# A two-layer decoder on one core: ten instead of seven weight tiles lead with their first token half in the second layer, shared large tiles in SBUF, and sums of squares on VectorE

## The chip, the core and the metric

The kernel runs on one core of a Trainium2 chip. The core has five engines with instruction streams of their own: TensorE (PE, matrix products into PSUM), VectorE (DVE), ScalarE (ACT), GpSimd (POOL) and SyncE (SP), which here only issues transfers between HBM and SBUF. The metric is the device time of one execution in microseconds (us), lower being better. A kernel is timed by the median of several executions; beside these, one execution was taken by the hardware profiler, and all views quoted below are of that one.

## The reference

A decoder of two layers runs over 528 tokens: 16 learned meta tokens ahead of a sequence of 512, each 1024 wide. The meta tokens are removed at the end. Everything is float32.

```python
for i in range(DEPTH):                                    # 2 layers
    m = _mixer(_rmsnorm(h, pre_mix_norm[i]), pos, w_in[i], ...)
    h = h + _rmsnorm(m, post_mix_norm[i])
    f = _conv_ffn(_rmsnorm(h, pre_ffn_norm[i]), ffn_up[i], ...)
    h = h + _rmsnorm(f, post_ffn_norm[i])
return h[:, N_META:]
...
def _mixer(...):
    rq, rk, rv, rg, gq, gk, gv, gr, ga = jnp.split(h @ w_in, offs, axis=-1)   # 3600 columns
    # retention: 4 heads of 128, rotary on rq and rk, fixed decay, chunkwise states
    # gated linear attention: 4 heads (64 for keys, 128 for values), decay from ga by a rank-16 gate
    merged = concat([headnorm(o_ret) * silu(rg), headrms(o_gla) * silu(gr)])
    return merged @ w_out
...
def _conv_ffn(h, ffn_up, ffn_conv_w, ffn_conv_b, ffn_down):
    a, g = jnp.split(causal_conv3(h @ ffn_up), 2, axis=-1)  # 2 x 2816 columns
    return (gelu(a) * g) @ ffn_down
```

## The kernel before

**Layout.** Activations stand transposed: features on the 128 partitions, tokens along the free dimension. The residual stream is `h`, eight slices (`KD`) of 128 features by 528 tokens (`L`) in float32. Each linear layer runs in float16 pieces: the normalised input `xh` and each weight are split into a high and a low half, and a product of a slice is three matmuls (high x high, low x high, high x low: lines 361 to 363). The tokens are cut in two halves, 0 to 232 and 232 to 528 (`SPLIT`). In layer 1 the first half of some tiles begins at token 14 (`base`), so it is 218 wide there. A weight tile of 128 columns with its eight slices makes 24 matmuls for a token half.

**Weights.** `plan()` lists all weight tiles in the order of use. `block()` hands out a tile and fetches up to ten tiles ahead (`AHEAD`): a load by SP into a staging buffer `st` (line 89), then ACT's high half (line 105) and DVE's low half (line 106) into a `unit`, of which there are ten (`UNITS`).

**Stages.** Each layer has a mixer, an output projection (`out_proj`, tile name po), an up-projection (`ffn_up`, pu) and a down-projection (`ffn_down` in layer 0, pd; `last_down` in layer 1, which works with seven products of quarter matrices). The mixer's projections have the tile name pj and run over 29 tiles in the order of `TILES`: ga, gk x2, gq x2, gv x4, then twice (rk x2, rq x2, rv x2), gr x4, rg x4. Each of them is done for both token halves.

**The lead.** The norm at the end of a layer gives the first token half of `xh` earlier than the second. So `mixer` makes a list `seq`: the first `LEAD` tiles for their first half, then the same tiles for their second half, then the other tiles with both halves in turn. Ahead of the first second half, whatever is left of the generator that makes the second half of `xh` is traced (`self.finish(self.later)`). `ffn_up` does the same with `ULEAD` = 5 pairs of tiles.

**The background.** Everything else of the mixer is written as generators in a list `bg`: `vtr` transposes a value tile, `gla(pr)` is a pair of gated-attention heads, `ret(hd)` a retention head (`ret_scores`: tiles rs and rst; `ret_states`: kv and sn; `head_out`: o, its statistics bst, mv, rs_t, rs_r, the normalised on, and the transposes pto, times the gate, into `merged`). `tick(n)` advances the first generator of the list that isn't waiting by one step, n times. In the mixer each half tile of `seq` ends with `tick(TICK)`, two steps. The two gated generators are spawned behind the second half of gq1, a retention head behind its rq, a transposition of v goes to the head of the list. What is left at the end of `seq` is done by `drain()`, ahead of the output projection. The output projection takes the slices of `merged` in the order 4, 5, 6, 7, 0, 1, 2, 3, so the retention heads last.

**The norm** (`norms`, `token_rstd`, `scaled`). ACT squares the eight slices one after another (line 330), and the squares are added up in `acc` (line 332): on POOL for slices 1 to 6, on DVE for slice 7, or always on DVE where the argument `last` is true. A matmul with ones sums over the partitions (nst, line 316); POOL takes the root (line 300); a matmul spreads it (nbc); DVE multiplies (line 345), POOL adds to `h` (line 347), the squares of the new `h` are summed in the same way, and `scaled` writes `xh` by ACT and DVE (lines 304 and 305).

**Space and order.** The SBUF pools give each tile an address from its life in a simulated run; where no number of buffers is given, the framework chooses it. The same simulated run puts the instructions of each engine in order. The order is kept as written at the start for ACT, DVE and SP (`manual_schedule`), and for the weight loads of layer 1 (`keep_in_program_order`). PSUM has three tiles for projections (`pmm`) and five for everything else (`pmx`). Two places in SBUF are used in turn by several tiles: the tag "xh" by `xh` and by `wrest` (part of the last down-projection's weights), and the pool `gen`, with 41 slots, by nearly all the short-lived tiles.

Of the kernel before, what the change touches and what calls it, by code (L numbers as in the profile page):

```python
# [14 lines left out]
P = 128  # L15
# [28 lines left out]
LEAD = 7  # L44
# [21 lines left out]
CELL = 1056  # L66

# [10 lines left out]
class Block:  # L78
# [8 lines left out]
    def load(self):  # L87
        st = self.st = cell(self.kern.stage, [P, self.nk, self.w], F32, *self.kern.stage_of(self.layer))
        load = self.kern.nc.sync.dma_start(st, self.src[:, self.c0 : self.c0 + self.w].rearrange("(k p) c -> p k c", p=P))
        if self.layer:  # L90
            self.kern.tc.keep_in_program_order(load)

    def fetch(self):
# [6 lines left out]
        if self.w < P:  # L100
            self.unit = cell(self.kern.wpool, [P, self.nk, P // (2 * self.w), 2, self.w], F16, "unit", "unit")
# [10 lines left out]
class Quarter:  # L112
# [21 lines left out]
    def fetch(self):  # L134
# [13 lines left out]
        self.unit = cell(kern.wpool, [P, 2, 2, 512], F16, "unit", "unit")[:, :, : self.nk]  # L148
# [6 lines left out]
class Kern:  # L155
    def __init__(self, ctx, tc, a):
# [5 lines left out]
        self.wpool = pool("wpool", UNITS)  # L162
# [7 lines left out]
        self.rate = 1  # L170

# [29 lines left out]
    def next_xh(self):  # L201
        xh = self.keep.tile([P, KD, 2, L], F16, tag="xh", name="xh", bufs=1)
# [7 lines left out]
    def w11_place(self, kk):  # L210
# [3 lines left out]
        if kk == WFIRST:  # L214
            self.wrest = self.keep.tile([P, HK - WFIRST, 512], F32, tag="xh", name="wrest", bufs=1)
        return self.wrest[:, kk - WFIRST : min(kk + 2, HK) - WFIRST]
# [11 lines left out]
    def constants(self):  # L228
        nc, a, c = self.nc, self.a, self.const
        widths = (("h", KD * L), ("ident", P), ("ones", P), ("mhalf", 10), ("par", NROW), ("pars", 48), ("cvec", 4 * 88), ("ss", 10), ("first", 10),  # L230
                  ("mask", len(LEVELS) * 16), ("decay", 2 * NH * 5), ("sso", 8))
        every = c.tile([P, sum(n for _, n in widths)], F32, name="every")
# [6 lines left out]
        self.decay = self.decay.rearrange("p (a h c) -> p a h c", a=2, h=NH)  # L239
        nc.gpsimd.memset(self.ones, 1.0)  # L240
# [32 lines left out]
    def mixer_constants(self):  # L273
# [4 lines left out]
        nc.sync.dma_start(self.decay, a["c_decay"])  # L278
        yield

    def tables(self):
        nc, a = self.nc, self.a
        self.cosT = self.g([P, L], F32, "cosT")
        self.sinT = self.g([P, L], F32, "sinT")
        self.tri = self.g([P, P + 16], F32, "tri")
        nc.sync.dma_start(self.cosT, a["c_cos"])
        nc.sync.dma_start(self.sinT, a["c_sin"])
        nc.sync.dma_start(self.tri, a["c_tri"])
# [894 lines left out]
```

## Time and profile before

| | before |
|---|---|
| median of three runs | 1273.3 us (1272.73 to 1276.95) |
| the profiled execution's own time | 1271.71 us |
| its span, from the first to the last instruction | 1269.8 us |
| mean granted clock of TensorE | 0.992 |
| HBM read, written | 120.45 MB, 2.10 MB |

The stages by the first matmul of each in the trace:

| stage | from, us | to, us |
|---|---|---|
| start | 0 | 13.7 |
| mixer of layer 0 | 13.7 | 243.7 |
| output projection of layer 0 | 243.7 | 289.8 |
| up-projection of layer 0 | 289.8 | 531.0 |
| down-projection of layer 0 | 531.0 | 653.8 |
| mixer of layer 1 | 653.8 | 879.8 |
| output projection of layer 1 | 879.8 | 923.5 |
| up-projection of layer 1 | 923.5 | 1158.5 |
| last down-projection and end | 1158.5 | 1269.8 |

How a page of the profile reads: its first part has the busy time, share of the span and number of instructions of each engine. "PEld" is the load of weights into TensorE, beside its matmuls. In a group's or an instruction's row, L662 is a line of the kernel, `rs<-rq,rk` the tile written and the tiles read (buffer numbers left out), 128x296 the partitions and elements, and x8 a count. A row of the timeline begins with the time from the start of the span and the length of the stretch, both in us, and may end with the idle time of the engine ahead of it and what ended that, in square brackets. In the table of groups the busy time and the mean in ns of one instruction stand behind the first bar, and the idle time with its releaser behind the second. The clock is the share of its full speed that TensorE was granted.

### The profile page before, as it was taken

To read this page: it belongs to the slowest core of one execution; us is meant where nothing else is said; L and a number is where in the kernel's file an instruction comes from. 1 tells how busy PE (TensorE), PEld (TensorE's weight loads), DVE (VectorE), ACT (ScalarE), POOL (GpSimd) and SP (SyncE) were. 2 spreads that over 40 slices of the span, in tenths; PEclk is the share of its full clock that TensorE was granted. 3 is DMA by queue.
4 is the path that set the end of the run, shared out by engine and by line. 5 is a ranking of instruction groups with operands and counts; after the bars stand their busy time and mean duration, and the time that the engine had idled before them with its cause. 6 is when DMAs were issued, how large, how long until landed. Compare 5 with 4: busy or idle time off the path is not lost.

```text
span 1269.8 us, 26401 instructions
## 1 busy us (share of the span) xinstructions
PE 1239.7 (98%) x11090; PEld 1019.8 (80%) x11090; DVE 819.8 (65%) x1510; ACT 642.0 (51%) x1200; POOL 167.6 (13%) x218
## 2 busy tenths in 40 slices
PE   8999999999999999999988999999999999999997
PEld 6777788888788888888876787888898888886443
DVE  5578845457876666512286688454478867887875
ACT  6664444354855555423255644343548656664541
POOL 1013310044000000000141132100430000000000
PEclk8999999999999999999998999999999999999999
DMA  9731222222433342214152322222215333304651
GB/s 258 212 87 55 68 67 67 68 72 63 133 102 98 101 125 79 88 47 120 32 139 67 84 68 68 64 68 71 84 50 146 108 102 103 126 1 165 200 191 67
DMA packets 206971, 124.26 MB, mean 98 GB/s; under 512 B 6704, under 2 KB 194276, under 8 KB 206852
## 3 DMA queue, kind: packets, MB, share of 16 engines
q1 hardware_dynamic: 206692, 122.04, 32.6%
q8 instruction: 87, 1.43, 0.5%
q0 software_dynamic: 160, 0.52, 0.2%
q14 instruction: 32, 0.26, 0.1%
HBM read 120.45 MB, written 2.10 MB: 97 GB/s over the span
## 4 chain that ended last, share of the span: by engine, by line
PE 80%; DVE 8%; ACT 3%; issue 3%; POOL 2%; DMA 1%; SPq 1%; DVEq 0%; POOLq 0%; ACTq 0%
PE pu L362 12%; PE pu L363 12%; PE pu L361 12%; PE pj L361 6%; PE pj L363 6%; PE pj L362 6%; PE pl L1047 5%; PE pd L362 3%; PE pd L361 3%; PE pd L363 3%; PE po L361 2%; PE po L362 2%; PE po L363 2%; DVE unit L106 2%; PE o L590 1%
## 5 line engine op out<-in xcount | busy, mean ns | idle before, releaser
L362 PE MATMUL pu<-xh,unit 128*128 128x296 f16 (+2 forms) x1408 | 385.7, 275 | 2.0 <-DVE xh L305 2.0
L363 PE MATMUL pu<-xh,unit 128*128 128x296 f16 (+2 forms) x1408 | 385.7, 275 | 0.0
L361 PE MATMUL pu<-xh,unit 128*128 128x296 f16 (+2 forms) x1408 | 384.0, 275 | 0.8 <-ACT xh L304 0.8
L106 DVE SCALAR_TENSOR_TENSOR unit<-st,unit 128x1024 f16<-128x1024 f32 (+1 forms) x186 | 227.5, 1226 | 214.5 <-ACT unit L105 207.8
L361 PEld LDWEIGHTS <-unit 128*128 128x128 f16 x2912 | 285.8, 98 | 48.8 <-issue 5.6
L363 PEld LDWEIGHTS <-unit 128*128 128x128 f16 x2912 | 285.6, 98 | 45.5 <-issue 2.9
L362 PEld LDWEIGHTS <-unit 128*128 128x128 f16 x2912 | 286.3, 98 | 44.5 <-issue 2.2
L105 ACT ACTIVATE unit<-st 128x1024 f16<-128x1024 f32 (+1 forms) x186 | 191.7, 1034 | 138.7 <-PE pu L363 48.7
L361 PE MATMUL pj<-xh,unit 128*128 128x296 f16 (+2 forms) x896 | 248.6, 279 | 1.8 <-ACT gaT L541 1.8
L363 PE MATMUL pj<-xh,unit 128*128 128x296 f16 (+2 forms) x896 | 248.8, 278 | 0.0
L362 PE MATMUL pj<-xh,unit 128*128 128x296 f16 (+2 forms) x896 | 248.6, 278 | 0.0
L934 ACT ACTIVATE u<-pu 128x296 f32<-128x296 f32 (+2 forms) x176 | 66.2, 379 | 99.3 <-PE pu L363 99.2
L363 PE MATMUL pd<-ffa,unit 128*128 128x232 f16 (+1 forms) x352 | 96.8, 276 | 0.0
L361 PE MATMUL pd<-ffa,unit 128*128 128x232 f16 (+1 forms) x352 | 96.8, 276 | 0.0
L362 PE MATMUL pd<-ffa,unit 128*128 128x296 f16 (+1 forms) x352 | 96.7, 276 | 0.0
L332 POOL TENSOR_TENSOR acc<-acc,sq 128x296 f32<-128x296 f32 (+2 forms) x36 | 32.4, 900 | 344.8 <-ACT sq L330 344.1
L300 POOL TENSOR_TENSOR rs_r<-rs_t,every 128x1 f32<-128x1 f32 (+5 forms) x33 | 37.2, 1131 | 279.5 <-DVE rs_t L297 99.5
L923 DVE SCALAR_TENSOR_TENSOR ca<-u,every,ca 128x527 f32<-128x527 f32 (+1 forms) x88 | 66.8, 759 | 10.8 <-ACT ca L918 9.6
L363 PE MATMUL po<-merged,unit 128*128 128x296 f16 (+2 forms) x256 | 69.9, 275 | 0.0
L362 PE MATMUL po<-merged,unit 128*128 128x296 f16 (+2 forms) x256 | 69.9, 275 | 0.0
L923 DVE SCALAR_TENSOR_TENSOR cg<-u,every,cg 128x527 f32<-128x527 f32 (+1 forms) x88 | 66.6, 757 | 4.9 <-ACT cg L918 4.3
L361 PE MATMUL po<-merged,unit 128*128 128x296 f16 (+2 forms) x256 | 69.6, 275 | 0.0
(218 smaller groups left out, 1535.6 us busy)
## 6 DMA issues: line engine op xcount, KB each, us to landing
st<-in_ffn_up SPq DMA_DIRECT2D x88, 512.0 KB, 3.8
st<-in_w_in SPq DMA_DIRECT2D x56, 512.0 KB, 4.0
st<-in_ffn_down SPq DMA_DIRECT2D x46, 512.0 KB, 3.9
st<-in_w_out SPq DMA_DIRECT2D x16, 512.0 KB, 3.6
st<-in_ffn_down SPq DMA_DIRECT2D x8, 384.0 KB, 5.5
out<-yo SPq DMA_DIRECT2D x8, 256.0 KB, 2.0
xt<-in_x SPq DMA_DIRECT2D x6, 256.0 KB, 3.6
w<-in_ffn_down SPq DMA_DIRECT2D x3, 512.0 KB
```

What stands on the lines that cost most here:

```text
L105: nc.scalar.activation(u[:, 0], st, AF.Copy, scale=SW)
L106: nc.vector.scalar_tensor_tensor(out=u[:, 1], in0=st, scalar=SW, in1=u[:, 0], op0=ALU.mult, op1=ALU.subtract)
L300: nc.gpsimd.tensor_tensor(out=r[:w, :n], in0=t[:w, :n], in1=self.mhalf[:w, :n], op=ALU.pow)
L332: eng.tensor_tensor(out=acc[:, :n], in0=acc[:, :n], in1=sq[:, :n], op=ALU.add)
L361: nc.tensor.matmul(ps[:, :n], w[:, 0, kk, :], x[:, 0, n0:n1], start=i == 0, stop=False)
L362: nc.tensor.matmul(ps[:, :n], w[:, 0, kk, :], x[:, 1, n0:n1], start=False, stop=False)
L363: nc.tensor.matmul(ps[:, :n], w[:, 1, kk, :], x[:, 0, n0:n1], start=False, stop=i == tot - 1)
L590: nc.tensor.matmul(o[:, i, :], intra(i), vn(i), start=i == 0, stop=i == 0, skip_group_check=i > 0)
L923: nc.vector.scalar_tensor_tensor(out=to, in0=u[:, max(lo, d) - d : L - d], scalar=self.cvec[:, ci(i) : ci(i) + 1], in1=to, op0=ALU.mult, o ...
L934: nc.scalar.activation(u[:, n0:n1], ps[:, : n1 - n0], AF.Copy, scale=IXW)
L1047: mm = lambda x, w, **kw: nc.tensor.matmul(ps, x, w, skip_group_check=more, **kw)
```

## The change

It has three parts.

*The lead.* `LEAD` becomes a pair: seven tiles lead in layer 0 as before, ten in layer 1 (ga, gk0, gk1, gq0, gq1, gv0 to gv3, rk0).

*Sums of squares.* In `ffn_down` all additions of squares go to VectorE; twelve of them were on GpSimd (six tiles, two token halves). `out_proj` stays as it was.

*Shared tiles.* Tiles that had places of their own or in the pool become views of a few large ones: `xroom` in `every` (the constants' tile) holds `xh`, and at the end `wrest` and `gbc`; `every` also takes `w2`, the staging of the narrow ga tile (`rank`), `tri` (loaded once, with the constants) and the rings of the small tiles rs_t, rs_r and sst. A tile `room` in each mixer holds the keys and queries `kq`, the tables cosT and sinT and the rings of vnt, mv, bst, ms, ont, dgrt and dgt; it has the tag "av", which the activations `av` of layer 0's `ffn_down` use too, now one tile instead of 22 slots. The output of `out_proj`, `m`, becomes one tile, whose place in layer 1 is later used for `late`; the early parts of layer 1's activations share one tile `f`. `ca` and `cg` of `ffn_up` share three buffers and `u` has ten (`2 * ULEAD`). The number of units is stated at each use instead of at the pool, and every unit and staging tile has the full size. The quarter blocks of w11 and t1 from the seventh slice on are fetched at most seven blocks ahead instead of eight.

```diff
-LEAD = 7
+LEAD = (7, 10)
...
+KINDS = (("rs_t", 10, 4), ("rs_r", 10, 4), ("sst", 1, 4))
+MIXKINDS = (("vnt", P, 6), ("mv", 20, 4), ("bst", 6, 8), ("ms", 10, 4), ("ont", P, 8), ("dgrt", 16, 4), ("dgt", 32, 2))
...
     def load(self):
-        st = self.st = cell(self.kern.stage, [P, self.nk, self.w], F32, *self.kern.stage_of(self.layer))
+        if self.w < P:
+            st = self.st = self.kern.rank.rearrange("p (k c) -> p k c", c=self.w)
+        else:
+            st = self.st = cell(self.kern.stage, [P, KD, self.w], F32, *self.kern.stage_of(self.layer))[:, : self.nk]
...
-            u = self.unit = cell(self.kern.wpool, [P, 2, self.nk, self.w], F16, "unit", "unit")
+            u = self.unit = cell(self.kern.wpool, [P, 2, KD, self.w], F16, "unit", "unit", UNITS)[:, :, : self.nk]
...
-        self.ahead = QAHEAD
+        self.ahead = QAHEAD if what not in ("w11", "t1") or kk < WFIRST else min(QAHEAD, WFIRST + 1)
...
     def next_xh(self):
-        xh = self.keep.tile([P, KD, 2, L], F16, tag="xh", name="xh", bufs=1)
+        xh = self.xroom.bitcast(F16).rearrange("p (k i n) -> p k i n", k=KD, i=2)
...
     def sm(self, shape, name, dt=F32, bufs=None):
-        return self.small.tile(shape, dt, tag=name, name=name, **({"bufs": bufs} if bufs else {}))
+        if name not in self.rings:
+            return self.small.tile(shape, dt, tag=name, name=name, **({"bufs": bufs} if bufs else {}))
+        room, at, size, count, used = self.rings[name]
+        self.rings[name][-1] += 1
+        at += used % count * size
+        t = room[: shape[0], at : at + math.prod(shape[1:])]
...
     def tables(self):
-        self.cosT = self.g([P, L], F32, "cosT")
-        self.sinT = self.g([P, L], F32, "sinT")
-        self.tri = self.g([P, P + 16], F32, "tri")
         nc.sync.dma_start(self.cosT, a["c_cos"])
         nc.sync.dma_start(self.sinT, a["c_sin"])
-        nc.sync.dma_start(self.tri, a["c_tri"])
...
     def mixer(self, l):
+        room = cell(self.keep, [P, 6 * L + sum(n * c for _, n, c in MIXKINDS)], F32, "av", "room", 1)
+        self.cosT, self.sinT = room[:, 4 * L : 5 * L], room[:, 5 * L : 6 * L]
+        self.ring(room[:, 6 * L :], MIXKINDS)
-        self.w2 = self.g([P, 256], F32, "w2")
...
-        kq = [cell(self.gen, [P, 2, L], F32, "kq", "kq", 2) for _ in range(2)]
+        kq = [room[:, 2 * L * pr : 2 * L * (pr + 1)].rearrange("p (i n) -> p i n", i=2) for pr in range(2)]
...
-        seq = [(t, 0) for t in TILES[:LEAD]] + [(t, 1) for t in TILES[:LEAD]] + [(t, hf) for t in TILES[LEAD:] for hf in range(2)]
+        lead = LEAD[l]
+        seq = [(t, 0) for t in TILES[:lead]] + [(t, 1) for t in TILES[:lead]] + [(t, hf) for t in TILES[lead:] for hf in range(2)]
         for i, ((nm, h), half) in enumerate(seq):
-            if i == LEAD:
+            if i == lead:
                 self.finish(self.later)
...
-        m = [self.g([P, L], F32, "m") for _ in range(KD)]
+        size = KD * L if l < DEPTH - 1 else HK * 2 * HT
+        self.room = cell(self.keep, [P, size], F32, "m%d" % l, "m", 1)
+        m = self.room[:, : KD * L].rearrange("p (k n) -> p k n", k=KD)
...
         def finish(col):
-            ca = self.g([P, L], F32, "ca")
-            cg = self.g([P, L], F32, "cg")
+            ca, cg = (cell(self.gen, [P, L], F32, "c", nm, 3) for nm in ("ca", "cg"))
...
-                t = self.g([P, 2, L], F16, "ffa")
-                self.split(t, cg[:, lo:], lo, L)
-                av.append(t)
+                if col == 0:
+                    keep["av"] = self.keep.tile([P, KF, 2, L], F16, tag="av", name="av", bufs=1)
+                self.split(keep["av"][:, col], cg[:, lo:], lo, L)
+                av.append(keep["av"][:, col])
...
     def ffn_down(self, l, av):
-        m = [self.g([P, L], F32, "m") for _ in range(KD)]
+        m = self.keep.tile([P, KD, L], F32, tag="m", name="m", bufs=1)
...
-                    self.sumsq(accs[half], ct, m[ct][:, n0:n1], n1 - n0, ct == KD - 1)
+                    self.sumsq(accs[half], ct, m[:, ct, n0:n1], n1 - n0, True)
```

More of the change, by code (lines that the diff above doesn't have):

```diff
@@ L170, in __init__ @@
         self.rate = 1
+        self.rings = {}
     def spawn(self, gen):
@@ L213, in w11_place, with ring @@
             return cell(self.keep, [P, 2, 512], F32, "w11", "w11", WFIRST // 2)
-        if kk == WFIRST:
-            self.wrest = self.keep.tile([P, HK - WFIRST, 512], F32, tag="xh", name="wrest", bufs=1)
-        return self.wrest[:, kk - WFIRST : min(kk + 2, HK) - WFIRST]
+        rest = self.xroom[:, : (HK - WFIRST) * 512].rearrange("p (k c) -> p k c", c=512)
+        return rest[:, kk - WFIRST : min(kk + 2, HK) - WFIRST]
     def sm(self, shape, name, dt=F32, bufs=None):
-        return self.small.tile(shape, dt, tag=name, name=name, **({"bufs": bufs} if bufs else {}))
+        if name not in self.rings:
[4 more added lines that the diff above has]
+        t = room[: shape[0], at : at + math.prod(shape[1:])]
+        names = "abc"[: len(shape) - 1]
+        return t if len(names) == 1 else t.rearrange(f"p ({' '.join(names)}) -> p {' '.join(names)}", **dict(zip(names, shape[1:])))
+    def ring(self, room, kinds):
+        at = 0
+        for name, size, count in kinds:
+            self.rings[name] = [room, at, size, count, 0]
+            at += size * count
     def mm(self, shape, name="mm"):
@@ L229, in constants @@
         nc, a, c = self.nc, self.a, self.const
-        widths = (("h", KD * L), ("ident", P), ("ones", P), ("mhalf", 10), ("par", NROW), ("pars", 48), ("cvec", 4 * 88), ("ss", 10), ("first", 10),
-                  ("mask", len(LEVELS) * 16), ("decay", 2 * NH * 5), ("sso", 8))
-        every = c.tile([P, sum(n for _, n in widths)], F32, name="every")
+        widths = (("h", KD * L), ("xroom", KD * L), ("ident", P), ("ones", P), ("mhalf", 10), ("par", NROW), ("pars", 48), ("cvec", 4 * 88), ("ss", 10), ("first", 10),
+                  ("w2", 256), ("rank", KD * 16), ("tri", P + 16), ("mask", len(LEVELS) * 16), ("decay", 2 * NH * 5), ("sso", 8), ("rooms", sum(n * c for _, n, c in KINDS)))
+        every = cell(c, [P, sum(n for _, n in widths)], F32, "every", "every")
         at = 0
@@ L278, in mixer_constants @@
         nc.sync.dma_start(self.decay, a["c_decay"])
+        nc.sync.dma_start(self.tri, a["c_tri"])
         yield
@@ L552, in v_natural @@
         w = 16 if ret is None else P
-        vnt = self.sm([w, P], "vnt", bufs=6)
+        vnt = self.sm([w, P], "vnt")
         pt = self.mx([P, 4, P], "ptv")
@@ L1032, in last_down @@
         nc = self.nc
-        gbc = [self.g([P, 512], F32, "gbc") for _ in range(2)]
+        c0 = (HK - WFIRST) * 512
+        gbc = [self.xroom[:, c0 + 512 * i : c0 + 512 * (i + 1)] for i in range(2)]
         for i in range(2):
```

32 lines of the change are left out of this document (17 added, 15 removed).

## The prediction, made before the changed kernel was run

> **What bounds the kernel now.** I read the page's first part, then a table of windows around the border of the two layers, then the timelines of single engines there and at the end of layer 1's mixer.
>
> ```profile
> PE 1239.7 (98%) x11090; PEld 1019.8 (80%) x11090; DVE 819.8 (65%) x1510; ACT 642.0 (51%) x1200; POOL 167.6 (13%) x218
> 533.00:553.00 20.00, 20.00 (x205) 19.71 (x202) 4.20 (x6) 4.25 (x10) 1.35 (x2) 1.00 0.09 27
> 566.00:590.00 24.00, 24.00 (x193) 18.65 (x191) 10.55 (x10) 11.80 (x16) 2.27 (x3) 1.00 0.68 179
> 880.00:884.40 4.40, 4.40 (x50) 4.40 (x48) 2.58 (x5) 1.25 (x3) 0.00 (x0) 1.00 0.27 76
> 672.00:677.20 5.20, 2.48 (x18) 1.74 (x17) 2.06 (x8) 1.16 (x3) 0.86 (x1) 1.00 0.00 0
> 677.20:684.10 6.90, 5.93 (x24) 3.43 (x24) 6.90 (x17) 4.46 (x9) 0.00 (x0) 0.51 0.02 4
> ...
> 672.30 0.66 PE L316 MATMUL nst<-every,acc 128*99 128x1 f32 x6
> 677.87 0.40 PE L540 MATMUL pj<-xh,unit 128*128 128x296 f16 x1 [1.69 <-ACT xh L304]
> ...
> 663.58 7.10 POOL L347 TENSOR_TENSOR every<-every,tmp 128x296 f32<-128x296 f32 x8 [3.01 <-DVE tmp L345]
> 681.79 1.60 DVE L305 TENSOR_TENSOR xh<-tmp,xh 128x296 f16<-128x296 f32 x4
> ```
>
> PE is the bound. In a window's row the length comes first, then busy time and count of PE, PEld, DVE, ACT and POOL, then clock, DMA share and GB/s. Windows of one width give the pace: 20.00/205 = 0.098 us for a 232-wide matmul, 24.00/193 = 0.124 for 296, 4.40/50 = 0.088 for 218. There is one real hole. Layer 1 leads with the first token half of seven tiles; they are done at 672. The second half's normalised input `xh` waits for POOL's eight residual adds (7.10 us from 663.58), a reciprocal root and its spreading. PE gets its first piece at 677.87 and the last ends on DVE at 681.79 + 1.60 = 683.4. Worse, the granted clock is 0.51 from 677.2 to 684.1: the idle window is paid for a second time.
>
> **The change part by part.**
>
> *Ten tiles lead in layer 1.* Three more first halves (gv2, gv3, rk0: 3 x 24 = 72 matmuls, all 232 wide) come ahead of the first second half: 72 x 0.098 = 7.0 us. Their weights are there:
>
> ```profile
> L105 ACT ACTIVATE unit<-st 128x1024 f16<-128x1024 f32 (+1 forms) x10 | 9.6, 973 | 8.4 <-PE pd L363 8.4
> ```
>
> that is ACT's group from 625 to 653, the ten units with which layer 1 begins. From 672.0 PE would run the 7.0 us and the small norm and gate matmuls of the window up to 677.2 (2.48 busy), to 681.5, or some 680.9 without their drains. The first 24 second-half matmuls then take 24 x 0.124 = 3.0 us at full clock, to 684: where the trace has done just those (x24 in the row from 677.20) at half clock. So all 72 are free: **-7.0 us**. `xh` may come 2 us later than now at no cost, as one of its eight pieces feeds ten or so matmuls of three open tiles. If a norm matmul stands too early in PE's order, up to 1 us comes back.
>
> *The same edit takes steps away from the background.* Attention runs in generators, and each half tile advances them by two steps. They begin behind gq1's second half. Now 47 half tiles follow from there on, 94 steps; with ten leading, 44, 88 steps. The generators need 90: two of gated attention with 21, four retention heads with 8, eight transposes of v with 2. So the four spare steps go, and the last retention head slips. The trace follows this count:
>
> ```profile
> 848.39 1.16 PE L662 MATMUL rs<-rq,rk 128*128 128x128 f32 x8
> 849.03 0.33 ACT L823 ACTIVATE gr<-pj 128x218 f32<-128x218 f32 x1
> 855.79 0.39 PE L677 MATMUL kv<-vn,kn 128*128 128x128 f32 x2
> 865.13 0.39 PE L677 MATMUL kv<-vn,kn 128*128 128x128 f32 x2
> 868.08 0.38 PE L597 MATMUL o<-vnt,dgrt 128*16 128x128 f32 x2
> 869.19 0.28 DVE L606 BATCH_NORM_STATS2 bst<-o 16x6 f32<-16x128 f32 x1
> 869.78 0.16 DVE L607 BATCH_NORM_AGGREGATE mv<-bst 16x2 f32<-16x6 f32 x1
> 870.60 0.16 DVE L297 TENSOR_TENSOR rs_t<-mv,every 128x5 f32<-128x5 f32 x1
> 870.84 1.28 POOL L300 TENSOR_TENSOR rs_r<-rs_t,every 128x5 f32<-128x5 f32 x1 [5.15 <-DVE rs_t L297]
> 872.15 1.37 DVE L626 TENSOR_SCALAR on<-o,mv,rs_r 128x128 f32<-128x128 f32 x4 [0.53 <-POOL rs_r L300]
> ...
> 879.07 0.60 PE L638 MATMUL pto<-every,on 128*128 128x128 f32 x4
> 879.78 0.89 DVE L641 SCALAR_TENSOR_TENSOR tmp<-pto,every,rg 128x256 f32<-128x256 f32 x2 [2.16 <-ACT rg L823]
> 880.53 0.72 ACT L304 ACTIVATE merged<-tmp 128x256 f16<-128x256 f32 x2
> 881.81 0.77 DVE L305 TENSOR_TENSOR merged<-tmp,merged 128x256 f16<-128x256 f32 x2
> 884.64 0.60 ACT L901 ACTIVATE m<-po 128x218 f32<-128x218 f32 x2 [3.39 <-PE po L363]
> ```
>
> Head 3's scores (848.39) stand right by gr3's first half (849.03), where the count puts them; its states (kv) begin at 855.79 behind rg0's first half, its output ends at 868.46, it is normalised by 873.8 and merely waits for the last gate until 879.07. With 88 steps its scores fall behind rg2's first half, its states behind rg3's first half, its output behind the last projection, its normalising behind everything. Call K the first kv. rg3's second half (24 x 0.124) and a kv end the projections at K + 3.4. kv rounds come 3.1 apart (855.79 to 865.13, three rounds), so the fourth is at K + 9.3 and o ends 3.3 later (865.13 to 868.46): K + 12.6 as paced now, K + 11 or so if rounds shorten once PE runs dry. What PE has meanwhile: sixteen o matmuls (by the rs row 1.16/8 each, 2.3), two kv rounds (0.4), and the output projection, which takes this head last: three open PSUM tiles x 7 of 8 slices x 3 = 63 x 0.088 = 5.5. So PE is dry at K + 11.6. Then follow, one behind another, 0.28, 0.16, 0.16, 1.28, two of the four normalisings 0.7, a transpose pair 0.3, and half of the last three rows before the copy of m (0.45, 0.36, 0.39): 4.1, with some nine handovers of 0.1 (as 870.76 to 870.84), 5.0. I take **+5.2 us** (4 to 7).
>
> *The clock* behind that wait: in the front hole a stretch of 3.4 us with 1.64 busy goes ahead of 6.9 us at 0.51:
>
> ```profile
> 673.80:677.20 3.40, 1.64 (x10) 1.14 (x11) 1.75 (x6) 0.80 (x2) 0.29 (x1) 1.00 0.00 0
> ```
>
> Those 6.9 us are two steps of some 3.4. One costs 1.7 us where PE has work, two 3.4, and part of it falls into the wait itself. I take **+1.0** (0 to 3.4). [...]
>
> *Sums of squares to VectorE* (ffn_down of layer 0).
>
> ```profile
> L332 POOL TENSOR_TENSOR acc<-acc,sq 128x296 f32<-128x296 f32 x6 | 5.8, 964 | 24.7 <-ACT sq L330 24.6
> L332 POOL TENSOR_TENSOR acc<-acc,sq 128x232 f32<-128x232 f32 x6 | 4.1, 675 | 270.9 <-ACT sq L330 270.9
> 641.10 3.47 DVE L332 TENSOR_TENSOR acc<-acc,sq 128x232 f32<-128x232 f32 x4
> 656.78 0.46 DVE L332 TENSOR_TENSOR acc<-acc,sq 128x296 f32<-128x296 f32 x1
> 646.69 0.57 PE L316 MATMUL nst<-every,acc 128*116 128x1 f32 x4 [1.26 <-DVE acc L332]
> ```
>
> Twelve adds move. Nine lie where nothing is late. The last three, of the second token half's tiles 4 to 6, fall at 640 to 646, where DVE's own adds take 0.87 (3.47/4) beside POOL, against 0.46 alone, and PE waits 1.26 for the last. Three more at 0.46 to 0.87 cost 1.4 to 2.6; POOL's absence gives back up to 4 x 0.41 = 1.6. I take **0** (-1.3, the whole wait, to +1.2). [...]
>
> *Shared tiles.*
>
> ```profile
> 653.07 0.35 SPq L287 DMA_DIRECT2D sinT<-in_c_sin  x1
> 653.98 84.73 SPq L89 DMA_DIRECT2D st<-in_w_in  x15
> 1000.00:1100.00 100.00, 100.00 (x921) 87.71 (x919) 74.95 (x100) 59.70 (x100) 0.00 (x0) 1.00 0.39 118
> 659.73 0.85 POOL L300 TENSOR_TENSOR rs_r<-rs_t,every 99x3 f32<-99x3 f32 x1 [10.20 <-DVE rs_t L299]
> 1158.73 3.86 DMA wrest<-in_ffn_down
> ```
>
> Layer 1's `room` (keys, tables, small rings) takes over the space of `av`, which is read until the last down product at 653. Behind its first write in SP's queue, the cosT load, stand sinT and the weight loads. They wait already: sinT goes at 653.07, weights at 653.98. cosT is first needed by rk0 near 680, so 0; if the loads slipped by more than 20 us, each would stall PE. POOL's memset of the keys waits for the same, with 10.20 us of idle time before its next work at 659.73. `rank`, `w2` and `tri` have space of their own (one load fewer): 0. ca and cg share three buffers, so cg's first pass on ACT waits for DVE's product of the column before, with PSUM copies behind it; both engines have slack (59.70 and 74.95 of 100) and three PSUM tiles (24 matmuls of 0.088 each) cover some 6 us. The load of `wrest` (1158.73) waits for the last reader of `xh` as before, or a few matmuls less. Together 0 (-1 to +2).
>
> **Sum**: -7.0 + 5.2 + 1.0 = -0.8 us. The profiled execution took 1271.7 (span 1269.8), the median is 1273.3; so 1270.9 by the first, **1272.5** as a median. A difference of 0.3%, 3.8 us, is about what a measurement of this kernel can tell from none.
>
> **Rivals.**
> 1. *The gain is kept*: head 3 finds enough cover at the end, if the last kv rounds run at 1 us instead of 3.1 and its chain ends under the 5.5 us of output projection. For it: today's head is normalised 5 us before its gate. Against it: the count, which the trace keeps to within a tile. -7.0 + 0.5: 1266.8. Chance 0.28.
> 2. *Slower*: the output projection finds no place in PE's order ahead of head 3's transposes, as today, where pto (879.07) stands before it. Then the 5.5 us of cover go, the wait is 10.7 and two half-speed windows follow: -7.0 + 10.7 + 3.4 = +7.1, less some 1.5 as kv rounds shorten: 1279. It decides from about 20 of the 63 matmuls behind the transposes on. Against it: today's first copy of m only comes at 884.64, behind some 52 po matmuls, so slices of a second and third tile were taken before the first was finished. 0.17.
> 3. *The lead does not do what it says*: PE's order puts the norm's matmuls and `xh` so that PE still waits, and half the 7.0 stays lost: +2.7, 1276. For it: PE waited 1.26 for nst at 646.69. Against it: nst at 672.30 hardly waited. 0.05.
>
> **How the numbers follow.** The forecast has 0.50 and its own range is 1269.5 to 1276.5 by the ends of its terms. Faster by over 0.3% (under 1269.5) is rival 1 and a little of the forecast: 0.30. Slower (over 1277.1) is rival 2 and the upper end of the others: 0.20. Within: 0.50. The range goes from 1265.5 to 1278.5 and leaves out the outer thirds of rivals 1 and 2.
>
> **What would show it.** The windows from 672 to 684 at 0.98 busy or more and a clock of 1.00; rs of the last head behind rg2's first half; a PE wait of 4 to 7 us on merged before po's eighth slice, with a half-speed window behind it. If PE shows no wait there, rival 1 holds; if po stands behind the transposes, rival 2. The prediction is wrong from the ground if layer 1's order follows readiness and not the count of steps.

## The result

The changed kernel takes 1285.26 us (median of four, 1284.51 to 1285.94) against 1273.01 for the one before (1271.69 to 1276.95 in the same comparison): a ratio of 1.0096, 95% interval 1.0078 to 1.0115. The profiled execution has a span of 1283.7 us after 1269.8. The forecast was 1272.5, with a range up to 1278.5; the change is 12 us slower, and outside it.

The first part of the page of the changed kernel, and a view of windows where the hole was (columns as in the prediction):

```profile
PE 1243.5 (97%) x11090; PEld 1021.8 (80%) x11090; DVE 827.8 (64%) x1522; ACT 640.4 (50%) x1200; POOL 160.3 (12%) x206
672.00:677.20 5.20, 5.20 (x56) 5.13 (x55) 1.46 (x6) 0.73 (x2) 0.85 (x1) 1.00 0.02 5
677.20:684.10 6.90, 6.90 (x63) 5.82 (x61) 5.79 (x15) 3.86 (x11) 0.00 (x0) 1.00 0.00 0
```

The hole is filled: both windows are fully busy at full clock, with 119 matmuls in place of 42. So the part of the forecast that was to gain time holds, and the loss is elsewhere. By the first matmul of each stage in the two traces:

| stage, us | before | after | difference |
|---|---|---|---|
| mixer of layer 0 | 230.0 | 232.2 | +2.2 |
| down-projection of layer 0 | 122.8 | 122.2 | -0.6 |
| mixer of layer 1 | 226.0 | 227.4 | +1.4 |
| output projection of layer 1 | 43.8 | 52.0 | +8.2 |
| last down-projection and end | 111.3 | 114.1 | +2.8 |
| the other four together | 536.0 | 535.8 | -0.2 |

The mixer of layer 1 and the projection behind it in three windows: up to the first second half, from there to the first matmul of the output projection, and the output projection. First the kernel before:

```profile
653.80:677.90 24.10, 19.35 (x189) 18.21 (x189) 17.57 (x43) 9.58 (x27) 8.81 (x10) 0.99 0.40 102
677.90:879.80 201.90, 198.60 (x1997) 162.79 (x1997) 132.81 (x347) 97.61 (x199) 34.33 (x50) 0.98 0.26 74
879.80:923.50 43.70, 43.70 (x401) 38.26 (x401) 20.86 (x37) 21.75 (x50) 18.72 (x22) 1.00 0.30 85
```

Then the changed kernel:

```profile
655.20:681.60 26.40, 25.84 (x261) 24.94 (x261) 18.27 (x45) 10.61 (x29) 8.84 (x10) 1.00 0.35 97
681.60:882.60 201.00, 190.44 (x1909) 154.13 (x1908) 128.65 (x327) 95.91 (x194) 35.72 (x49) 0.97 0.26 75
882.60:934.60 52.00, 49.88 (x419) 42.02 (x418) 24.52 (x53) 22.09 (x52) 19.91 (x23) 0.93 0.25 72
```

The first window takes 2.3 us more and holds 72 matmuls more, which are 7.0 us of work: 4.7 us are won there, and 3.4 us more as the half-speed stretch of the hole is gone. **The middle window is the surprise.** It has 88 matmuls fewer (the 72, and 16 of the last head that moved behind it). 201.9 less 7.0 (72 x 0.098), some 2 for the 16, and 3.4 for the clock is 189.5; it takes 201.0. PE's idle time there goes from 3.3 (201.90 - 198.60) to 10.6 us (201.00 - 190.44), which is 7.3 us. And there are half-speed stretches of another kind, three of some 3.4 us, which cost about 5 us together:

```profile
724.60:728.00 3.40, 3.27 (x45) 2.31 (x44) 3.40 (x9) 2.08 (x4) 1.00 (x1) 0.66 0.00 0
790.20:793.60 3.40, 2.41 (x12) 1.50 (x13) 3.37 (x9) 2.15 (x5) 1.18 (x2) 0.55 0.48 144
814.00:820.80 6.80, 6.80 (x46) 5.21 (x45) 0.07 (x1) 2.31 (x10) 0.00 (x0) 0.75 0.01 2
```

Who ends PE's waits is in the view of waits over layer 1's mixer and output projection (behind the colon: us in total, times, longest). In the mixer before, PE's waits on lps from 706 to 782 us come to 0.3 and 0.3; below them the changed kernel's longest three:

```profile
PE lps L738 <- DVE lvx L788: 0.3, 1, 0.3
PE lps L738 <- DVE tots L795: 0.3, 1, 0.3
...
PE lps L756 <- ACT lvx L805: 5.3, 6, 1.6
PE pj L558 <- ACT every L322: 1.7, 1, 1.7
PE pto L656 <- DVE on L644: 1.5, 1, 1.5
```

lps are the level scores of gated attention (`level_scores`): seven levels, each a chain of ScalarE's copy, VectorE's difference (both lvx), GpSimd's and VectorE's multiplications, and PE. They make two stretches, one for each pair of heads. Windows from the first lps of a stretch to the last, before:

```profile
718.20:737.20 19.00, 18.85 (x309) 14.52 (x308) 17.39 (x42) 10.39 (x19) 7.58 (x10) 1.00 0.21 57
761.60:780.00 18.40, 17.22 (x291) 13.13 (x290) 17.78 (x45) 10.71 (x24) 6.28 (x8) 1.00 0.20 59
```

and in the changed kernel:

```profile
721.20:746.60 25.40, 23.34 (x335) 17.53 (x334) 23.07 (x54) 11.38 (x21) 10.73 (x15) 0.93 0.23 64
773.00:795.70 22.70, 17.02 (x281) 12.21 (x280) 19.64 (x47) 8.82 (x16) 10.03 (x13) 0.92 0.16 48
```

The second stretch has ten matmuls fewer than before and lasts 4.3 us longer, 5.7 of its 22.7 us idle. Before, it ran beside rv1, rk2 and the first half of rk3; now it runs beside rq2 and rq3, and the rotary work (`rope`, on VectorE, ScalarE and GpSimd) of rk3 and rq2 falls into it: GpSimd has 10.03 us of work there after 6.28. The first stretch holds 26 matmuls more, and is longer by more than these: 2.1 us of it are idle (25.40 - 23.34). The generators moved against the tiles by several half tiles, and this is what the forecast had not looked at.

The end went as the count had said. In the timelines of PE and the windows around it:

```profile
870.42 1.16 PE L680 MATMUL rs<-rq,rk 128*128 128x128 f32 x8
877.94 0.49 PE L695 MATMUL kv<-vn,kn 128*128 128x128 f32 x2
891.73 1.28 PE L656 MATMUL pto<-every,on 128*128 128x128 f32 x4 [1.50 <-DVE on L644]
893.89 0.71 PE L379 MATMUL po<-merged,unit 128*128 128x218 f16 x3 [0.61 <-ACT merged L322]
...
890.20:893.60 3.40, 1.58 (x6) 0.83 (x6) 2.33 (x7) 0.18 (x1) 1.03 (x1) 0.91 0.00 0
893.60:900.40 6.80, 6.51 (x40) 5.50 (x40) 1.08 (x3) 2.74 (x9) 1.29 (x2) 0.55 0.01 2
```

The last head's scores stand behind rg2's first half, its states behind rg3's, and PE has 63 po matmuls ahead of its transposes. The wait is 1.5 + 0.6 us, and a stretch of 6.8 us at about half clock follows a window that was 1.58 of 3.40 us busy. 2.1 of waiting, some 3.4 of clock and 18 matmuls more (419 after 401) make the 8.2 us.

### The profile page after: what moved, and what is told of

The parts are those of the page before. It is cut to its first block, busy times and chain, and to the rows that moved or that the text cites. A ratio compares the mean times of both kernels' runs of the same rounds, so it can differ in the third digit from the quotient of the medians.

```text
span 1283.7 us, 26385 instructions
## 1 busy us (share of the span) xinstructions
PE 1243.5 (97%) x11090; PEld 1021.8 (80%) x11090; DVE 827.8 (64%) x1522; ACT 640.4 (50%) x1200; POOL 160.3 (12%) x206
## 4 chain that ended last, share of the span: by engine, by line
PE 78%; DVE 10%; DMA 4%; ACT 3%; issue 2%; POOL 2%; SPq 1%; DVEq 0%; POOLq 0%; ACTq 0%
PE pu L380 12%; PE pu L381 12%; PE pu L379 12%; PE pj L379 6%; PE pj L380 6%; PE pj L381 6%; PE pd L379 3%; PE pd L381 3%; PE pd L380 3%; DMA st<-in_ffn_down 2%; PE po L379 2%; PE po L380 2%; PE po L381 2%; PE pl L1072 2%; DVE unit L111 1%
## 5 line engine op out<-in xcount | busy, mean ns | idle before, releaser
L380 PE MATMUL pu<-every,unit 128*128 128x296 f16 (+2 forms) x1408 | 385.4, 274 | 2.1 <-DVE every L323 2.1
L381 PE MATMUL pu<-every,unit 128*128 128x296 f16 (+2 forms) x1408 | 385.4, 274 | 0.0
L379 PE MATMUL pu<-every,unit 128*128 128x296 f16 (+2 forms) x1408 | 383.7, 274 | 0.7 <-ACT every L322 0.7
L111 DVE SCALAR_TENSOR_TENSOR unit<-st,unit 128x1024 f16<-128x1024 f32 x184 | 228.9, 1244 | 170.4 <-ACT unit L110 164.9
L110 ACT ACTIVATE unit<-st 128x1024 f16<-128x1024 f32 x184 | 191.6, 1042 | 157.6 <-PE pu L381 52.7
L379 PE MATMUL pj<-every,unit 128*128 128x296 f16 (+2 forms) x896 | 249.5, 279 | 2.7 <-ACT gaT L559 2.2
L380 PE MATMUL pj<-every,unit 128*128 128x296 f16 (+2 forms) x896 | 249.9, 279 | 0.0
L381 PE MATMUL pj<-every,unit 128*128 128x296 f16 (+2 forms) x896 | 249.5, 279 | 0.0
L381 PE MATMUL pd<-av,unit 128*128 128x232 f16 (+1 forms) x352 | 96.9, 276 | 0.0
L380 PE MATMUL pd<-av,unit 128*128 128x296 f16 (+1 forms) x352 | 96.7, 276 | 0.0
L379 PE MATMUL pd<-av,unit 128*128 128x232 f16 (+1 forms) x352 | 96.7, 276 | 0.0
L350 DVE TENSOR_TENSOR acc<-acc,sq 128x296 f32<-128x296 f32 (+2 forms) x60 | 33.7, 564 | 77.9 <-ACT sq L348 75.6
L318 POOL TENSOR_TENSOR every<-every 128x1 f32<-128x1 f32 (+5 forms) x33 | 37.3, 1135 | 296.1 <-DVE every L315 118.8
L1072 PE MATMUL pl<-unit,fk 128*128 128x512 f16 x330 | 71.5, 379 | 2.8 <-ACT part L1082 2.8
L379 PE MATMUL po<-merged,unit 128*128 128x296 f16 (+2 forms) x256 | 70.9, 280 | 0.6 <-ACT merged L322 0.6
L380 PE MATMUL po<-merged,unit 128*128 128x296 f16 (+2 forms) x256 | 71.4, 280 | 0.0
L381 PE MATMUL po<-merged,unit 128*128 128x296 f16 (+2 forms) x256 | 71.3, 280 | 0.0
```

Source lines behind the costliest of these rows:

```text
L110: nc.scalar.activation(u[:, 0], st, AF.Copy, scale=SW)
L111: nc.vector.scalar_tensor_tensor(out=u[:, 1], in0=st, scalar=SW, in1=u[:, 0], op0=ALU.mult, op1=ALU.subtract)
L318: nc.gpsimd.tensor_tensor(out=r[:w, :n], in0=t[:w, :n], in1=self.mhalf[:w, :n], op=ALU.pow)
L350: eng.tensor_tensor(out=acc[:, :n], in0=acc[:, :n], in1=sq[:, :n], op=ALU.add)
L379: nc.tensor.matmul(ps[:, :n], w[:, 0, kk, :], x[:, 0, n0:n1], start=i == 0, stop=False)
L380: nc.tensor.matmul(ps[:, :n], w[:, 0, kk, :], x[:, 1, n0:n1], start=False, stop=False)
```

## The experiments

Two theories stood at first. **A**: the first halves that lead are missing later as cover, so ten leading tiles cost the time by themselves. **B**: the shared tiles tie the attention's steps together and cause the waits. Each time is a median, with its ratio to the kernel before timed beside it (1272.7 to 1274.6).

**The parts alone.** The lead alone, on the kernel before: `LEAD = (7, 10)`, indexed by the layer.

> The kernel before with ten tiles leading in layer 1 and nothing else changed. Theory A (the three first halves are taken from the work that covers the gated attention's level scores and the end of the mixer): the mixer and output projection of layer 1 take some 9.7 us more than before, as in the changed kernel, so 1273.0 + 9.7 = 1282.7 us; the waits of PE on lps are there again. Theory B (the shared tiles tie the attention's steps together and cause these waits): the gain of 7 us is kept apart from the last head's wait, 1272 to 1275 us, and PE hardly waits on lps.

1279.29 us, 1.0055 (1.0039 to 1.0072). In the profile the mixer and output projection of layer 1 take 228.6 + 51.7, 10.5 more than before; this execution was the slowest of six (1277.57 to 1282.57). The median lies between the two expected numbers, nearer theory A's.

The changed kernel with `LEAD = (7, 7)`:

> The changed kernel with seven tiles leading in layer 1: shared tiles and sums remain. Theory A: mixer and output projection of layer 1 as before (269.7 us together), the hole at 672 to 684 is back; what is left is the start (+2.1), the last stage (+2.8) and the sums (-0.6): 1273.0 + 4.3 = 1277.3 us. Theory B: the waits on lps stay, with the hole beside them: 1273.0 + 4.3 + 9.7 = 1287 us or more.

1277.25 us, 1.0036 (1.0023 to 1.0048). Start and last stage stay long (mixer of layer 0 233.5, last stage 113.6). Its two stretches of level scores last 19.0 and 19.9 us, with no wait on lps over 0.33 us. So theory B falls and A stands. By these two medians the lead costs 6.6 us (1279.29 - 1272.72) and all the rest 4.5 (1277.25 - 1272.72), together 11.1 of the 12.

The sums alone, on the kernel before, and the changed kernel with the sums back on GpSimd:

```diff
-self.sumsq(accs[half], ct, ..., n1 - n0, ct == KD - 1)
+self.sumsq(accs[half], ct, ..., n1 - n0, True)
```

> The kernel before with the twelve additions of squares on VectorE and nothing else. By the stage times of the changed kernel the down-projection of layer 0 gets 0.6 us shorter and the wait for nst (1.26 us before) goes: 1272.4 us. A rival: DVE is late with the normalising behind it, 1273.0 to 1274 us.

> The changed kernel with the twelve additions back on GpSimd. By the stage times: 1285.3 + 0.6 = 1285.9 us, with a wait of some 1.3 us for nst near 646. If the sums matter in layer 1's mixer (DVE work that comes later there), it would be 2 us or more faster than the changed kernel.

1271.01 us, 0.9985 (0.9973 to 0.9996), and 1287.98, 1.0119 (1.0100 to 1.0137): the sums are worth more than the 0.6 us expected. The down-projection takes 121.3 alone (122.8 before), 123.6 with the sums back. In the view of groups over the down-projection, VectorE's adds of the first token half before:

```profile
L332 DVE TENSOR_TENSOR acc<-acc,sq 128x232 f32<-128x232 f32 x8 | 5.8, 731 | 6.8 <-ACT sq L330 6.5
```

and with the sums alone:

```profile
L332 DVE TENSOR_TENSOR acc<-acc,sq 128x232 f32<-128x232 f32 x14 | 6.5, 467 | 44.7 <-ACT sq L330 44.4
```

Six adds more cost VectorE 0.7 us. These means mix adds with and without company. The three adds that ran beside GpSimd's additions of squares, and the three at that place with the sums alone (in ns: shortest, median, longest):

```profile
L332 DVE TENSOR_TENSOR acc<-acc,sq x3: 834/1007/1053, 642.6 to 645.6; 128x232 f32<-128x232 f32 x3
L332 DVE TENSOR_TENSOR acc<-acc,sq x3: 393/399/400, 642.1 to 644.1; 128x232 f32<-128x232 f32 x3
```

The wait for nst is gone. The three adds that run beside GpSimd's additions to `h` take as long with the sums alone as before (0.51, 0.78 and 0.87 us before, 0.50, 0.77 and 0.87 after).

**Where the steps stand.** Ten leading tiles on the kernel before, and more steps for the background early on:

```diff
+early = l == DEPTH - 1 and LEAD[l] + 4 < i < 2 * LEAD[l]
-self.tick(TICK)
+self.tick(2 * TICK if early else TICK)
```

> The kernel before with ten leading tiles, and with four steps of the background instead of two behind the five leading second halves that follow gq1 (ten more steps in all). Theory C (what costs the time is the place of the attention's steps: two more half tiles pass before gated attention begins, its second pair's level scores then fall beside the rotary tiles rk2 to rq3, and the last head slips behind the projections): the output projection of layer 1 is back at 43.8 us, PE's waits on lps near 785 to 790 go, the hole stays filled: 1272.7 - 7 = 1266 us (1264 to 1269). Theory A (the first halves are cover that is missing later, wherever the steps stand): the waits turn up at another place, 1277 to 1281 us.

1269.71 us, 0.9979 (0.9969 to 0.9989). The output projection is back at 43.8 us, the mixer at 223.3. Theory A falls: the cover is not missing everywhere, it depends on where the steps stand. Some of the gain stays lost (1266 was expected, 1269 at most): the stretches last 19.9 and 21.6 us, with a wait of 1.4 in the second. With the sums:

> The same with the twelve additions of squares on VectorE: 1.7 us less than the run before it by either theory, so 1264 us by theory C and 1278 by theory A.

1268.44 us, 0.9964 (0.9952 to 0.9977).

Next, ten leading tiles with rv2 and rv3 ahead of rk2, rk3, rq2 and rq3 in layer 1:

```diff
+TILES = (TILES, TILES[:15] + [TILES[i] for i in (19, 20, 15, 16, 17, 18)] + TILES[21:])
```

> The kernel before with ten leading tiles, and in layer 1 the value tiles rv2 and rv3 ahead of rk2, rk3, rq2 and rq3. The steps are as many as in the kernel with the lead alone, and the last head still ends behind 63 matmuls of the output projection; only what stands beside the second pair's level scores changes (rv tiles, which ScalarE empties, in place of rotary tiles, which VectorE and GpSimd work on). If the neighbours matter, the waits of that stretch (5.4 us and a half-speed window of 1.7) go: 1279.3 - 6 = 1273 us. If only the count does, it stays near 1279.

1274.03 us, 1.0010 (1.0001 to 1.0020). The middle window and the second stretch with the lead alone, then the middle window and both stretches of this kernel:

```profile
681.20:882.00 200.80, 188.81 (x1918) 153.40 (x1916) 130.21 (x330) 95.89 (x195) 35.20 (x49) 0.99 0.26 75
773.90:796.90 23.00, 17.35 (x281) 12.22 (x280) 19.98 (x47) 8.82 (x16) 9.63 (x13) 0.93 0.16 47
...
681.20:872.40 191.20, 185.13 (x1908) 151.97 (x1907) 126.68 (x327) 95.32 (x193) 34.33 (x49) 1.00 0.28 78
720.80:746.10 25.30, 21.80 (x334) 16.82 (x334) 23.00 (x53) 11.29 (x21) 10.70 (x15) 1.00 0.23 64
772.60:790.20 17.60, 17.09 (x293) 13.04 (x292) 15.96 (x40) 9.45 (x20) 6.65 (x8) 1.00 0.21 61
```

The middle takes 191.2 us after 200.8, near the 189.5 worked out above: all but two of the lost microseconds come back by an order of tiles alone (one of them because ten matmuls less stand in the window). The first stretch stays as long as it was, so they come back in the second stretch and behind it. The reason was not quite the expected one. The second stretch starts behind rv3 and runs beside rk2 and rk3, not beside value tiles; but the work of rq2 and rq3 is out of it, and GpSimd has 6.65 us there. The end stays long (output projection 53.1).

Eight leading tiles:

> The kernel before with eight leading tiles. One half tile of 2.4 us goes into the hole, the last head's output stands ahead of rg3, so the output projection stays at 43.8 us. Without a loss in between: 1272.7 - 2.4 = 1270.3 us, 1 or 2 less if it also spares a half-speed window. If the second pair's level scores beside rotary tiles cost what they did with ten (5 to 7 us): 1275 to 1277.

1278.61 us, 1.0043 (1.0031 to 1.0056), more than either number. In its profile the hole is not gone (waits of 1.3 and 1.0 us at 676 and 678, half clock from 680 to 685) and the second stretch is already long (24 us). A little lead has the cost and not the gain.

Both edits of the order in one: rv2 and rv3 first, and three steps beside the gr tiles of layer 1 (`TICK + 1 if l and nm == "gr" else TICK`), on the kernel before with the sums, and on the changed kernel:

> The kernel before with ten leading tiles, rv2 and rv3 ahead of rk2 to rq3, three steps in place of two beside the gr tiles of layer 1 (eight more in all), and the squares' additions on VectorE. In the order of its instructions the last head is done at rg2. The mixer of layer 1 takes 218.0 + 2.5 (the last head's matmuls come back from the output projection), the output projection 43.8 us: 264.3 in place of 269.8, and 1.5 less for the sums: 1272.9 - 7 = 1266 us. If the extra steps put the retention heads too close together, waits of 2 to 4 us on their states: 1268 to 1270.

> The changed kernel with the same two edits of the order (rv2 and rv3 first, three steps beside the gr tiles of layer 1). If the place of the attention's steps is what the ten leading tiles cost, its mixer and output projection of layer 1 come to about 265 us in place of 279.4: 1285.3 - 14.5 = 1271 us; what is then left against the best order of the kernel before, 4 to 6 us, belongs to the shared tiles (start and last stage). If shared tiles bring waits of their own into the mixer, 1275 us or more.

1268.64 us, 0.9962 (0.9950 to 0.9975), and 1273.57, 1.0007 (0.9998 to 1.0016). The first has the higher time that was named, but no wait of 2 us on the retention heads' states; mixer and output projection take 267.6 us where 264.3 were expected. The changed kernel gets back 11.7 us by its order alone, of the 14.5 expected; in the profile, mixer and output projection of layer 1 take 221.7 + 43.8 = 265.5, as expected. Its two stretches last 25.3 and 17.6 us, as in the kernel without shared tiles.

**Why the stretch is longer.** Two runs with the lead alone moved work of the rotary tiles of layer 1 between VectorE and GpSimd: the multiplication by sinT to GpSimd, or the addition to VectorE.

> The kernel with the lead alone, where in layer 1 the second multiplication of the rotary tiles (with sinT) is on GpSimd in place of VectorE. The two stretches of level scores last 25.3 and 23.1 us with the lead alone (19.0 and 18.4 before), about what VectorE's own instructions in them add up to (27.3 and 23.9; 22.1 and 21.8 before). If VectorE's load sets their length, they get shorter by about half of the rotary work in them (5.6 and 3.9 us), so 2.8 + 2 = 4.8 us less: 1279.3 - 4.8 = 1274.5. If the chain through GpSimd sets it (the level's multiplication waits behind the rotary additions), the added GpSimd work makes it 1279 to 1283.

> The kernel with the lead alone, where in layer 1 the last addition of the rotary tiles is on VectorE in place of GpSimd: the mirror of the run that gave GpSimd a multiplication more (second stretch 26.0 us after 23.1, and no faster). If the level's chain through GpSimd sets the length (its multiplication by the totals waits behind rotary additions of 1.2 us each), the second stretch gets 2 to 4 us shorter and a half-speed window may go: 1275 to 1277 us. If VectorE's load sets it, it gets longer by what VectorE gains (four additions, some 2 us): 1281 to 1283.

1284.25 us, 1.0092 (1.0078 to 1.0105), and 1282.82, 1.0073 (1.0056 to 1.0090): neither is faster. The two stretches with the multiplication on GpSimd:

```profile
720.60:743.80 23.20, 20.01 (x311) 15.27 (x311) 21.13 (x47) 11.22 (x21) 14.94 (x19) 0.93 0.17 48
771.90:797.90 26.00, 20.50 (x289) 14.20 (x287) 19.38 (x44) 9.36 (x17) 12.63 (x17) 0.80 0.14 42
```

and with the addition on VectorE:

```profile
720.90:749.40 28.50, 24.24 (x335) 18.31 (x334) 23.69 (x59) 11.68 (x22) 6.39 (x9) 0.88 0.21 57
775.50:797.10 21.60, 17.08 (x280) 12.57 (x279) 19.49 (x51) 8.47 (x16) 5.48 (x9) 0.92 0.17 50
```

With the lead alone the stretches are 25.3 and 23.0 us. GpSimd relieved (5.48 us) shortens the second by 1.4, GpSimd loaded (12.63) lengthens it by 3.0. The first goes the other way: with VectorE loaded and one matmul more (334 before) it is 3.2 longer. But much of this is clock: the 26.0 us are at 0.80 with eight matmuls more, the 28.5 at 0.88, and PE's idle time in them (5.5 and 4.3 us) is near that with the lead alone (5.7 and 3.5). So moving rotary work from one of the two engines to the other doesn't help, and these two runs don't show which engine sets the length. A last run kept rv2 and rv3 first, but sent their transpositions to the end of the background's list (`self.bg.insert(len(self.bg), ...)`):

> The kernel with ten leading tiles and rv2 and rv3 first, but their transpositions go to the end of the background's list and take no step from the second pair of gated heads. If the stretch was shortened (17.6 us in place of 23.1) because the transpositions stretched the levels over more half tiles, it goes back to 21 to 24 us and the time to about 1278. If it was the tiles beside it, it stays at 17 to 19 us and the time near 1274.

1278.63 us, 1.0038 (1.0025 to 1.0051). Its second stretch:

```profile
772.10:790.90 18.80, 16.13 (x283) 11.86 (x283) 17.06 (x42) 7.69 (x14) 5.62 (x8) 1.00 0.20 58
```

The stretch stays short, which speaks for the neighbours, but the time is that of the other theory: PE idles 2.7 us in the stretch (18.80 - 16.13) in place of 0.5, and the mixer takes 223.5 us after 218.0. The stretch itself is only 1.2 us longer, so most of that arises elsewhere. The tiles beside the levels count, and so does the place of the transpositions; these runs don't divide the loss between the two.

**The shared tiles.** On the kernel before, the quarter blocks fetched seven ahead:

```diff
-self.ahead = QAHEAD
+self.ahead = QAHEAD if what not in ("w11", "t1") or kk < WFIRST else min(QAHEAD, WFIRST + 1)
```

> The kernel before with the quarter blocks of w11 and t1 from the seventh slice on fetched seven blocks ahead in place of eight, and nothing else. If this is what lengthens the last stage of the changed kernel (114.1 us after 111.3), the last stage is 113.5 to 114 here too: 1272.9 + 2.5 = 1275.4 us. If it is the place of wrest in the shared tile (its load comes later), the last stage stays at 111.3: 1272.9.

1276.31 us, 1.0021 (1.0010 to 1.0032); the last stage takes 114.2, as in the changed kernel. PE's longest wait there in the timelines of the kernel before, of this one, and of the changed one:

```profile
1187.90 4.48 PE L1047 MATMUL pl<-unit,fk 128*128 128x512 f16 x20 [0.71 <-ACT part L1057]
```

```profile
1189.97 2.42 PE L1047 MATMUL pl<-unit,fk 128*128 128x512 f16 x7 [2.02 <-ACT part L1057]
```

```profile
1201.11 2.10 PE L1072 MATMUL pl<-unit,fk 128*128 128x512 f16 x9 [2.83 <-ACT part L1082]
```

With one block less fetched ahead, the last units of the first products are made later, and ACT's copies of those products (part), which stand behind them in ACT's order, begin at 1189.35 us in place of 1187.27 and release PE later. Of the 2.9 us, 1.3 are this wait; the rest is a half-speed stretch behind it:

```profile
1190.80:1194.20 3.40, 3.40 (x9) 1.21 (x8) 2.54 (x3) 1.31 (x3) 0.00 (x0) 0.51 0.00 0
```

In the changed kernel the wait is 2.1 us longer than before, of 2.8 us in all, and no half-speed stretch follows (the clock is 1.00 from 1201.1 to 1215 us). So the shorter fetch by itself makes the last stage as long as in the changed kernel.

For the start, the changed kernel with the edited order and the loads of cosT, sinT and tri issued by GpSimd:

> The changed kernel with the two edits of the order, and with the loads of cosT, sinT and tri issued by GpSimd in place of SP. If they delay the gains' rows in SP's queue (first transpose of them at 48.1 us after 44.1, with 2.35 us of waiting), the mixer of layer 0 goes from 232.9 to about 230.5 us: 1273.6 - 2.4 = 1271.2. If the transfers themselves are what delays the rows, it stays at 232 to 233.

1272.77 us, 0.9987 (0.9974 to 0.9999), and 230.6 us for the mixer of layer 0: the number came, but not from the place named. PE's first transpose of the gains' rows, before, in the changed kernel, and in this run:

```profile
44.13 0.25 PE L265 MATMUL ptc<-every,rows 68*128 68x68 f32 x1 [0.83 <-DMA rows<-in_gla_gate_b]
```

```profile
48.11 0.28 PE L286 MATMUL ptc<-every,rows 68*128 68x68 f32 x1 [2.35 <-DMA rows<-in_gla_norm_w]
```

```profile
47.80 0.25 PE L287 MATMUL ptc<-every,rows 68*128 68x68 f32 x1 [2.13 <-DMA rows<-in_ffn_conv_w]
```

The rows are as late as in the changed kernel. So the tables in SP's queue are not what delays them. SP's own timeline shows what does, again before, in the changed kernel and in this run:

```profile
34.78 2.89 SPq L89 DMA_DIRECT2D st<-in_w_in  x2
37.72 1.44 SPq L257 DMA_DIRECT2D rows<-in_post_mix_norm  x1
...
34.60 6.77 SPq L94 DMA_DIRECT2D st<-in_w_in  x4
41.47 1.80 SPq L278 DMA_DIRECT2D rows<-in_post_mix_norm  x1
...
34.55 7.11 SPq L95 DMA_DIRECT2D st<-in_w_in  x4
41.76 1.56 SPq L279 DMA_DIRECT2D rows<-in_post_mix_norm  x1
```

Eighteen weight loads stand ahead of the rows in all three, and the rows go when the last of them has gone, some 4 us later with shared tiles. Before, two of the last fourteen go at 16.19 us, among the loads of `gla_gate_w`; with shared tiles all fourteen stand behind these, from 18.52 us on (19.97 in this run). Why the simulated order puts them there isn't shown. The 2.3 us of this run come mostly from the clock: from 30 to 40 us it has 1.00 and 97 matmuls, where the same kernel with the tables on SP has 0.81 and 77.

**An order without rotary neighbours.** The kernel before with ten leading tiles, the early steps, the sums, and the value tiles ahead of the rotary ones in both groups:

> The kernel before with ten leading tiles, four steps behind the last five leading second halves of layer 1, the squares' additions on VectorE, and layer 1's value tiles ahead of the rotary ones in both groups (rv0, rv1 behind rk0; rv2, rv3 ahead of rk2). By the place of the steps both stretches of level scores stand mostly beside value tiles: 18 to 20 us each (25.3 and 17.6 with rv2 and rv3 alone), and the last head is done at rg0: mixer of layer 1 219 to 221 us, in all 1264 to 1266. If the value tiles don't help the first stretch, 1268 as the two best so far.

1268.22 us, 0.9956 (0.9943 to 0.9969). The second stretch is 21.1 us, beside rq1, rv2 and rv3, so the order didn't do all that was expected. Three kernels with an edited order and the sums on VectorE end within half a microsecond of each other (1268.2 to 1268.6); each beats both kernels, the one before by 4.4 to 6.4 us, of which the sums alone are worth 1.7.

## Why the prediction was wrong

- *The hole* (-7.0): right. Both windows are full, at full clock; 4.7 us of matmuls and 3.4 of clock are won, and the middle of the mixer gets shorter where the order lets it (191.2 us with rv2 and rv3 first).
- *The background's steps* (+5.2, clock +1.0): right in the count and in its places, to the half tile and to the 63 matmuls. Wait and clock measure 2.1 + 3.4 = 5.5 after 6.2. That the sum is so near is in part luck: the wait was less than half of its term and the clock more than three times its own. Counted from the first kv at 877.94, the last head's output was done at K + 11.2, near the fast end of the forecast; PE ran dry at K + 12.3, not 11.6; and 1.6 us of what was left were the transposes' own work. No run shows the +1.0 for the clock: the half-speed stretch (6.80 us at 0.55) was paid in full, some 3.4 us.
- **The step that failed** is the sentence "So the four spare steps go, and the last retention head slips". The count was followed to the end of the list only. Every step behind gq1 shifts against the tiles, and the forecast never asked what stands beside each step, so the shift had no price in its sum. It took PE as the bound all through the middle; but in the first stretch of level scores VectorE is busy for 17.39 of 19.00 us beside PE's 18.85, so there is little room for other work, and the shift brings VectorE's work there to 23.07 us. The shift cost some 11 us (201.0 after 189.5), as 7.3 us of waiting and about 5 of half clock; an exchange of tiles wins back nearly all of it (200.8 to 191.2 us). That the place of the steps is the cause is shown by the runs that change the order and nothing else; which engine makes the stretches longer is not shown. None of the rivals named it.
- *Sums* (0, from -1.3): the size. The lower end was right: -1.5 in the stage, -1.7 as a median. The three adds beside GpSimd's additions of squares took 2.9 us, the three at that place take 1.2 without them: 1.7 us came back where the forecast counted up to 1.6. It priced the three moved adds at 0.46 to 0.87 us each; adds of their form took 464 ns (128x296, the mean of six with the sums alone), its lower end. The adds beside the GpSimd additions that stay cost what they had cost before, and the slow ones (834 to 1053 ns) had stood beside those that moved.
- *Shared tiles* (0, -1 to +2): too small. The changed kernel with seven leading tiles is 4.5 us slower than the kernel before, though its sums save 1.7. The last stage (+2.8) comes from the shorter fetch, which the forecast left without a price. At the start (+2.2), PE's longer wait for the gains' rows is 1.5 (2.35 after 0.83); the forecast looked at SP's queue at the border of the layers, not here.
- *The range*: "by the ends of its terms" is not what those ends add up to. They give 1268.0 to 1279.9 us in place of 1269.5 to 1276.5, and the measured time lies outside that too.

Sum of the terms by the profiled executions: +2.3 (first window), -0.9 (middle), +8.3 (output projection), +2.2, +2.8, -0.6 and -0.2 are the 13.9 us between the spans.

## What to carry to other kernels

Where background work is advanced by a count, a change of the foreground's order moves every one of its steps: lay the two lists side by side from the first step to the last, and look in each stretch for every engine that is nearly full there, not only for the one that bounds the kernel. Work taken forward to fill a hole is a gain only if what it covered before still finds cover, and a few steps more or two tiles exchanged can decide that. A fetch distance shortened by one is an edit with a price of its own (2.9 us in the last stage here).

## What was not expected of the hardware

The half-speed stretches came behind windows that were far from idle: 1.58 of 3.40 us busy ahead of 6.80 us at 0.55. The prediction had read the first such case in the kernel before and counted on one behind the last wait; it did not expect three more in the middle of the mixer (0.66, 0.55 and 0.75 in the windows quoted with the result), behind windows with 1.65 to 1.97 of 3.40 us busy.

Where such a stretch falls differed between two executions of the same tiles. The lead alone and the kernel with rv2 and rv3 first have the same tiles up to the first second half of layer 1; from the mixer's first matmul to it, the trace of the one takes 28.8 us and that of the other 27.2. In the one the clock falls on the way, in the other it does not (first the lead alone):

```profile
656.40:659.80 3.40, 3.40 (x20) 2.70 (x19) 2.98 (x9) 1.53 (x4) 0.00 (x0) 0.51 0.00 0
656.40:659.80 3.40, 3.40 (x38) 3.35 (x37) 3.36 (x11) 1.53 (x4) 0.00 (x0) 1.00 0.00 0
```

The six executions of the lead alone go from 1277.57 us, at a mean granted clock of 0.993, to 1282.57 at 0.989; 0.004 of 1280 us is 5.1 us, about the difference. What sets the place of such a stretch is not shown here: behind 0.58 of 3.40 us busy (1197.7 to 1201.1 us of the changed kernel) the clock stayed at 1.00.

And a VectorE add of 128x232 took 834 to 1053 ns beside GpSimd's additions of squares, and 393 to 400 ns at that place with these moved to VectorE.
